# First mixer of a two-layer encoder: eight convolution taps on ScalarE, summed by adding transfers, and weight units split without VectorE

## The chip, the cores and the metric

The kernel runs on one core of one Trainium2 chip. The metric is the device time of one launch in microseconds, as the median of several runs. A profile of one further execution gives the rows below. In profiles, PE is TensorE, PEld its weight loads, DVE VectorE, ACT ScalarE, POOL GpSimd and SP SyncE, whose queue issues most transfers.

## The reference

1024 tokens of width 1024 pass two layers. Each layer is a mixer and a SwiGLU feed-forward, with a residual, scaled by 4^0.25, and a layer normalization after each:

```python
def conv_lru_mixer(x, ...):                       # layer 0
    h = x @ w_in + b_in                           # 1024 -> 4 x 512
    a_val, a_gate, b_gate, b_rec = split(h, 4)
    ya = silu(layer_norm(causal_depthwise_conv(a_val * sigmoid(a_gate), conv_w, conv_b), ...))  # 31 taps
    yb = rg_lru(causal_depthwise_conv(b_rec, lru_conv_w, lru_conv_b), ...) * gelu(b_gate)       # 4 taps
    return concatenate([ya, yb]) @ w_out
x = layer_norm(alpha * x + mixer(x), ...)         # layer 1: differential attention
x = layer_norm(alpha * x + (silu(x @ w_gate) * (x @ w_up)) @ w_down, ...)
```

All data are float32.

## The kernel before

Every matrix operand is split in two parts: `hi` is the value rounded to TensorE's fast float32 form (fp32r), made by a copy on ScalarE, and `lo` is the value less `hi`, made by a subtraction on VectorE (`split`, L569). A product is three matmuls: hi hi, hi lo, lo hi (`three`). Weights come in units of 128 x 1024 (512 KB): `load` (L551) issues the load of a unit, `ready` (L561) splits it, `prefetch` keeps up to `cap` units ahead. The first mixer loads 40 units, 24 of `win` and 16 of `wout0`.

The tokens are worked in two halves of 512. `PLAN` (L394) is the order of the steps of the first mixer:

```python
PLAN = "c0 c1 R0 R1 R2 R3 c2 L0 L1 L2 L3 c3 k3 G0 G1 G2 G3 D S x m v s o y Q0 Q1 Q2 Q3 B0 B1 B2 B3 O H0 H1 H2 H3"
```

`c` (`conv_in`, L982) multiplies value and gate for 128 channels of both halves, gates them (`glu`) and convolves the first half; `R` and `Q` are the recurrent input of the two halves with its four-tap convolution, `L` its gates, `G` and `H` the GeLU gates, `D` and `S` decay and scan, `m`, `v`, `s`, `o` mean, variance, scaling and splitting of the convolved half, `B` the 31-tap convolution of the second half, and `O` the output projection of the first half with its normalization. The feed-forward of the first half follows (`operands_a`, `ffn_lead` L1182, 18 of 22 steps), with the rest of the second half's mixer between, then mean, variance and output projection of the second half. `ffn_lead` makes two weight operands of each `up` unit: the sum of its two halves, added on GpSimd, and the second half.

`conv31` (L774) gives the last 8 to 13 of 31 taps to ScalarE or GpSimd as multiplications and adds their products on GpSimd into a page of its own; the first 18 to 23 taps are multiply-adds on VectorE into two accumulators, which two more additions join. Its pages are six halves of a fixed ring (`cring`).

SBUF is a pool of 35 pages of 128 x 1024, first free first used (`alloc` L463, `halloc` L470 for halves); a page's new user waits for all users of the old one. The order of instructions on each engine is fixed when the program is built: `solve` (L240) gives each operation a cost and a due time and lists it on its engine; a transfer issued by GpSimd is taken to hold GpSimd for 1000 ns and to begin 700 ns later. The engine then runs its list in order, and waits where an operand is not there.

Of the kernel before, what the change touches and what calls it, by code (L numbers as in the profile page):

```python
# [22 lines left out]
HALF = 512  # L23
# [3 lines left out]
HALO = 32  # L27
NSMALL = 856
# [54 lines left out]
class Order:  # L83
# [156 lines left out]
    def solve(self):  # L240
# [50 lines left out]
        while done < n:  # L291
# [29 lines left out]
            if o.dma:  # L321
                if e == "pool":
                    free[e] = s + 1000
                    b = free[e] + 700
                else:
                    free[e] = s + 60
                    hw = max(hw, s + 25) + 450
                    b = hw + 650
# [68 lines left out]
class Trunk:  # L397
    def __init__(self, tc, io, order=None, lead0=18, lead1=18, ratio1=1.65, ratio2=0.62, pool_a=(13, 13, 12, 8), pool_b=9,
                 own=(6, 6, 6, 0), ropes=2, early=3, stay=4, plan=PLAN):
# [8 lines left out]
        self.plan, self.own = plan, own  # L408
        self.pool_a, self.pool_b = pool_a, pool_b
# [8 lines left out]
        self.ahead = 1  # L418
        self.kinds = ("win", "wout0")
# [131 lines left out]
    def load(self, key):  # L551
        u = Unit(self.alloc())
        src = self.unit_src(key)

        cuts = (0, HALF, PG) if self.next_load < 2 else (0, PG)
        u.cuts = [slice(a, b) for a, b in zip(cuts, cuts[1:])]
# [4 lines left out]
    def ready(self, u):  # L561
        if u.hi is None:
            u.hi, u.lo = self.alloc(True), self.alloc(True)
            for c in u.cuts:
                self.split(self.pr(u.hi)[:, c], self.pr(u.lo)[:, c], self.pg(u.raw)[:, c])
            self.release(u.raw)
            self.unsplit -= 1

# [76 lines left out]
    def layer_norm(self, r, g, b, spread=False, store=None, parts=1):  # L645
# [7 lines left out]
        nc.gpsimd.tensor_scalar(mv[:, 2:3], mv[:, 1:2], EPS, 1.0, ALU.add, ALU.mult)  # L653
# [120 lines left out]
    def conv31(self, i, h, npool):  # L774
# [4 lines left out]
        o = self.cv(h, i)  # L779
        off = HALO * h  # L780

        def wcol(s):
            return self.vec("even_conv_w", (30 - s) * 4 + i)

        def span(s):
            a = 0 if h else s
            return slice(a, HALF), g[:, off + a - s:off + HALF - s]

        pages = [self.cring[n % len(self.cring)] for n in range(self.cnext, self.cnext + 4)]
        self.cnext += 4  # L790
        o2, p, *q = pages
        acc = [o, self.pg(o2)]
        nd = 31 - npool
        if h == 0:
            nc.vector.memset(acc[1][:, 0:1], 0.0)
            nc.gpsimd.memset(self.pg(p)[:, 0:nd], 0.0)
        for s in range(nd):
            sl, src = span(s)
            ov = acc[s % 2][:, sl]
            if s == 0:  # L800
                nc.vector.tensor_scalar(ov, src, wcol(s), self.vec("even_conv_b", i), ALU.mult, ALU.add)
            elif s == 1:
                nc.vector.tensor_scalar(ov, src, wcol(s), 0.0, ALU.mult, ALU.add)
            else:
                nc.vector.scalar_tensor_tensor(ov, src, wcol(s), ov, ALU.mult, ALU.add)
        for n, s in enumerate(range(nd, 31)):
            sl, src = span(s)
            t = self.pg(p if n == 0 else q[n % 2])[:, sl]
            if h == 0 and n < self.own[i]:
                nc.gpsimd.tensor_scalar(t, src, wcol(s), 0.0, ALU.mult, ALU.add)  # L810
            else:
                nc.scalar.activation(t, src, AF.Identity, scale=wcol(s))
            if n:
                pv = self.pg(p)[:, sl]
                nc.gpsimd.tensor_tensor(pv, pv, t, ALU.add)
        nc.vector.tensor_add(o, o, acc[1])
        nc.vector.tensor_add(o, o, self.pg(p))
# [17 lines left out]
    def conv_var(self, h):  # L835
# [4 lines left out]
        nc.gpsimd.tensor_tensor(a, v[0], v[0], ALU.mult)  # L840
# [50 lines left out]
    def lru_decay(self, h):  # L891
# [11 lines left out]
        for i in range(4):  # L903
            q = self.halloc()
            a = self.pg(self.la[i])
            nc.gpsimd.tensor_tensor(self.pg(q), a, a, ALU.mult)
# [1018 lines left out]
```

## Time and profile before

| | |
|---|---|
| median of 3 runs | 2374.13 us (2370.38 to 2376.66) |
| profiled execution, its own time | 2371.16 us |
| span of its trace | 2369.4 us |
| TensorE busy | 2195.5 us, 93% |
| VectorE busy | 1936.4 us, 82% |
| GpSimd busy | 1166.5 us, 49% |
| ScalarE busy | 981.2 us, 41% |
| mean granted TensorE clock | 0.967 of full speed |

The busy times of different engines overlap. A group of instructions is written as line, engine, operation, tile written and tiles read; nearly all have one line, since a helper records every operation. `g` are pages of the pool, `xt` the split tokens, `PS` accumulators, `SM` small columns. "x39 | 52.0, 1349 | 2.5 <-ACT" is 39 instructions, busy 52.0 us, 1349 ns each on average, and 2.5 us of idle time just before them, ended by ScalarE.

### The profile page before, as it was taken

How to read it: one execution, taken by the hardware profiler on the slowest of the kernel's cores; microseconds unless marked ns; L12 is line 12 of the kernel's file. 1: busy time of each engine (PE TensorE's matmuls, PEld its weight loads, DVE VectorE, ACT ScalarE, POOL GpSimd, SP SyncE). 2: the span in 40 equal slices, each digit the busy share in tenths (PEclk: the TensorE clock that was granted, in tenths of full speed). 3: DMA queues.
4: the chain of work that ended last, by engine and by line, in shares of the span. 5: the costliest groups of instructions: out<-in, count | busy, mean ns of one | idle time of the engine just before them, and what ended most of it. 6: DMA issues, size and time to landing. Idle time of an engine off the chain costs nothing.

```text
span 2369.4 us, 28804 instructions
## 1 busy us (share of the span) xinstructions
PE 2195.5 (93%) x9856; PEld 1760.1 (74%) x9856; DVE 1936.4 (82%) x2681; ACT 981.2 (41%) x1733; POOL 1166.5 (49%) x880
## 2 busy tenths in 40 slices
PE   9677987889999989979999998999998999999995
PEld 7566865668888868868787776677676888887884
DVE  8999997898767578987688877777779777768897
ACT  5246344433333244334344554455554333334431
POOL 4642346248766554661243435232236777656463
PEclk9888998999999999989999999899999999999998
DMA  5013233445444576756544557445436544476674
GB/s 173 31 45 116 90 131 117 151 151 219 155 150 160 187 252 157 191 132 216 175 129 152 166 173 226 133 143 169 133 98 227 189 162 157 150 230 206 177 178 129
DMA packets 149411, 374.70 MB, mean 158 GB/s; under 512 B 16144, under 2 KB 32784, under 8 KB 149264
## 3 DMA queue, kind: packets, MB, share of 16 engines
q1 hardware_dynamic: 136592, 349.78, 44.2%
q0 software_dynamic: 12672, 23.07, 5.8%
q8 instruction: 78, 1.28, 0.2%
q14 instruction: 69, 0.57, 0.1%
HBM read 291.01 MB, written 81.79 MB: 157 GB/s over the span
## 4 chain that ended last, share of the span: by engine, by line
PE 63%; DVE 20%; DMA 8%; issue 4%; POOL 2%; ACT 2%; SPq 0%; DVEq 0%; ACTq 0%; POOLq 0%
PE PS L378 63%; DVE g L378 16%; DMA g<-in_down 3%; DVE SM L378 2%; ACT g L378 2%; POOL g L378 2%; DMA g<-a_d 2%; DVE xt L378 1%; DMA g<-in_win 1%; POOL SM L378 1%; DMA z_d<-g 1%; DMA g<-in_up 0%; DMA q_d<-g 0%; DMA g<-q_d 0%; SPq L378 0%
## 5 line engine op out<-in xcount | busy, mean ns | idle before, releaser
L378 POOL TENSOR_TENSOR g<-g,g 128x512 f32<-128x512 f32 (+6 forms) x461 | 730.3, 1595 | 573.0 <-ACT g L378 293.4
L378 PE MATMUL PS<-xt,g 128*128 128x512 f32 x2416 | 624.0, 406 | 48.7 <-DVE g L378 28.4
L378 PE MATMUL PS<-g,xt 128*128 128x512 f32 (+3 forms) x2768 | 636.6, 380 | 4.1 <-DVE g L378 3.7
L378 PE MATMUL PS<-xt 128*128 128x512 f32 x2240 | 590.3, 391 | 12.4 <-ACT xt L378 8.5
L378 PEld LDWEIGHTS PS<-g,xt 128*128 128x128 f32 (+1 forms) x2768 | 504.1, 189 | 117.3 <-issue 11.7
L378 PEld LDWEIGHTS PS<-xt,g 128*128 128x128 f32 x2416 | 456.8, 193 | 167.1 <-DVE g L378 40.1
L378 DVE TENSOR_TENSOR xt<-g,xt 128x512 fp32r<-128x512 f32 x532 | 508.2, 981 | 62.9 <-ACT xt L378 59.7
L378 DVE TENSOR_TENSOR g<-g,g 128x512 f32<-128x512 f32 (+2 forms) x463 | 455.2, 997 | 71.5 <-ACT g L378 47.0
L378 ACT CAST xt<-g 128x512 fp32r<-128x512 f32 x532 | 313.7, 619 | 458.6 <-PE PS L378 274.7
L378 PEld LDWEIGHTS PS<-xt 128*128 128x128 f32 x2240 | 420.5, 188 | 105.8 <-ACT xt L378 10.6
L378 DVE TENSOR_TENSOR g<-PS,g 128x512 f32<-128x512 f32 (+3 forms) x408 | 257.8, 641 | 175.4 <-POOL g L378 81.9
L378 POOL TENSOR_TENSOR g<-g 128x512 f32<-128x512 f32 x153 | 231.2, 1528 | 264.6 <-DMA g<-in_gate 119.5
L378 PE MATMUL PS<-g,g 128*128 128x512 f32 (+6 forms) x984 | 257.9, 387 | 54.2 <-ACT g L378 25.3
L378 ACT CAST g<-g 128x512 fp32r<-128x512 f32 (+1 forms) x247 | 187.1, 771 | 287.4 <-DVE g L378 101.8
L378 PE MATMUL PS<-xt,xt 128*128 128x512 f32 (+4 forms) x736 | 255.6, 400 | 3.0 <-ACT xt L378 1.2
L378 PEld LDWEIGHTS PS<-g,g 128*128 128x128 f32 (+1 forms) x984 | 172.6, 193 | 100.0 <-ACT g L378 27.1
L378 DVE SCALAR_TENSOR_TENSOR g<-g,SM,g 128x1024 f32<-128x1024 f32 (+9 forms) x215 | 241.2, 1133 | 5.9 <-POOL SM L378 3.1
L378 ACT ACTIVATE g<-PS,SM 128x512 f32<-128x512 f32 (+8 forms) x266 | 179.3, 688 | 153.3 <-PE PS L378 95.0
L378 PEld LDWEIGHTS PS<-xt,xt 128*128 128x128 f32 (+1 forms) x736 | 135.6, 190 | 43.1 <-issue 12.2
L378 PE MATMUL PS<-SM,g 128*128 128x128 f32 (+1 forms) x704 | 115.6, 281 | 26.7 <-DVE g L378 16.2
L378 PEld LDWEIGHTS PS<-SM,g 128*128 128x128 f32 x704 | 91.4, 158 | 49.7 <-DVE g L378 17.1
L378 POOL DMA_DIRECT2D g<-in_down x88 | 79.0, 951 | 97.4 <-DMA g<-in_down 88.4
(48 smaller groups left out, 1101.4 us busy)
## 6 DMA issues: line engine op xcount, KB each, us to landing
g<-in_up SPq DMA_DIRECT2D x88, 512.0 KB, 4.4
g<-in_down SPq DMA_DIRECT2D x176, 256.0 KB, 3.3
z_d<-g SPq DMA_DIRECT2D x44, 512.0 KB, 3.6
g<-z_d SPq DMA_DIRECT2D x44, 512.0 KB, 4.2
g<-in_gate SPq DMA_DIRECT2D x44, 512.0 KB, 4.2
g<-in_down POOLq DMA_DIRECT2D x88, 256.0 KB, 6.5
a_d<-g SPq DMA_DIRECT2D x36, 512.0 KB, 4.8
g<-a_d SPq DMA_DIRECT2D x36, 512.0 KB, 5.9
```

The source lines that it names most:

```text
L378: r = f(*a, **k)
```

## The change

- `conv31`: the same for both halves and all channels. ScalarE makes the products of the first eight taps, each in a temporary half page from the pool; the first is written into the accumulator with the bias, the other seven are added into it by transfers from SBUF to SBUF, issued by GpSimd (`accum_op=ALU.add`). The other 23 taps are VectorE's. The fixed ring has four halves instead of six, and `conv31` of the first half stands one product later.
- `ready`: for all units but the first two of the first mixer, ScalarE writes `hi` and then `-hi` into `lo`, and a transfer issued by GpSimd adds the raw unit (512 KB) to `lo`.
- `ffn_lead`, in both layers: the sum of the two halves of an `up` unit is made by an adding transfer from DRAM (256 KB) into the first half.
- The square in `conv_var` and the four in each `lru_decay` move from GpSimd to ScalarE, and the addition of epsilon in `layer_norm` from GpSimd to VectorE.
- The planner takes a transfer issued by GpSimd to begin 1500 ns after its issue instead of 700.

```diff
@@ Order.solve
                 if e == "pool":
                     free[e] = s + 1000
-                    b = free[e] + 700
+                    b = free[e] + 1500
@@ Trunk.load
         u = Unit(self.alloc())
+        u.adding = self.adding
...
+        if self.next_load == 1:
+            self.adding = True
@@ Trunk.ready
             u.hi, u.lo = self.alloc(True), self.alloc(True)
+            if u.adding:
+                self.split_adding(u)
+                self.unsplit -= 1
+                return
...
+    def split_adding(self, u):
+        nc = self.nc
+        nc.scalar.copy(self.pr(u.hi), self.pg(u.raw))
+        nc.scalar.mul(self.pr(u.lo), self.pg(u.hi), -1.0)
+        nc.gpsimd.dma_start(self.pg(u.lo), self.pg(u.raw), accum_op=ALU.add)
+        self.release(u.raw)
@@ Trunk.layer_norm
-        nc.gpsimd.tensor_scalar(mv[:, 2:3], mv[:, 1:2], EPS, 1.0, ALU.add, ALU.mult)
+        nc.vector.tensor_scalar(mv[:, 2:3], mv[:, 1:2], EPS, 1.0, ALU.add, ALU.mult)
@@ Trunk.conv31 (NTAP = 8)
+        acc = [self.cv(h, i)] + [self.pg(self.cring[(self.cnext + n) % len(self.cring)]) for n in range(2)]
+        self.cnext += 2
...
+        for s in range(NTAP):
+            sl, src, w = tap(s)
+            if s == 0:
+                nc.scalar.activation(acc[0], src, AF.Identity, bias=self.vec("even_conv_b", i), scale=w)
+                continue
+            t = self.halloc()
+            nc.scalar.activation(self.pg(t)[:, sl], src, AF.Identity, scale=w)
+            nc.gpsimd.dma_start(acc[0][:, sl], self.pg(t)[:, sl], accum_op=ALU.add)
+            self.release(t)
+        for s in range(NTAP, 31):
+            n = s - NTAP
+            sl, src, w = tap(s)
+            ov = acc[1 + n % 2]
+            if n < 2:
+                if h == 0:
+                    nc.vector.memset(ov[:, 0:s], 0.0)
+                nc.vector.tensor_scalar(ov[:, sl], src, w, 0.0, ALU.mult, ALU.add)
             else:
-                nc.vector.scalar_tensor_tensor(ov, src, wcol(s), ov, ALU.mult, ALU.add)
-        for n, s in enumerate(range(nd, 31)):
-            sl, src = span(s)
-            t = self.pg(p if n == 0 else q[n % 2])[:, sl]
-            if h == 0 and n < self.own[i]:
-                nc.gpsimd.tensor_scalar(t, src, wcol(s), 0.0, ALU.mult, ALU.add)
-            else:
-                nc.scalar.activation(t, src, AF.Identity, scale=wcol(s))
-            if n:
-                pv = self.pg(p)[:, sl]
-                nc.gpsimd.tensor_tensor(pv, pv, t, ALU.add)
-        nc.vector.tensor_add(o, o, acc[1])
-        nc.vector.tensor_add(o, o, self.pg(p))
+                nc.vector.scalar_tensor_tensor(ov[:, sl], src, w, ov[:, sl], ALU.mult, ALU.add)
+        nc.vector.tensor_add(acc[1], acc[1], acc[2])
+        nc.vector.tensor_add(acc[0], acc[0], acc[1])
@@ Trunk.conv_var
-        nc.gpsimd.tensor_tensor(a, v[0], v[0], ALU.mult)
+        nc.scalar.activation(a, v[0], AF.Square)
@@ Trunk.lru_decay
-            nc.gpsimd.tensor_tensor(self.pg(q), a, a, ALU.mult)
+            nc.scalar.activation(self.pg(q), a, AF.Square)
@@ Trunk.layer0_in
-        self.cring = [self.halloc() for _ in range(6)]
+        self.cring = [self.halloc() for _ in range(4)]
@@ Trunk.conv_in
         self.glu(i, 0, bv, bg)
-        self.conv31(i, 0, self.pool_a[i])
         bv = self.bank()
         self.colmul(bv, uv, 1)
+        self.conv31(i, 0)
         bg = self.bank()
@@ Trunk.ffn_lead
             pu, u1, u2 = self.raw("up", l, f)
-            w2, w4 = self.w_operand(u1, u2), self.w_operand(u2)
+            nc.gpsimd.dma_start(u1, self.io["up"][l][f][:, HALF:], accum_op=ALU.add)
+            w2, w4 = self.w_operand(u1), self.w_operand(u2)
@@ Trunk.emit, ahead of layer 1's first loads
                 self.cap = 4
+                self.adding = False
```

## Rows read from the trace of the kernel before

**Rows 1.** Page, part 1: busy us of each engine, share of the span, instructions.

```profile
PE 2195.5 (93%) x9856; PEld 1760.1 (74%) x9856; DVE 1936.4 (82%) x2681; ACT 981.2 (41%) x1733; POOL 1166.5 (49%) x880
```

**Rows 2.** Table by stretch: start:end, length, engines' busy us, clock, DMA share, GB/s.

```profile
0.00:95.00 95.00, 89.60 (x382) 73.29 (x383) 87.77 (x100) 43.72 (x60) 55.01 (x44) 1.00 0.35 121
95.00:181.00 86.00, 51.63 (x203) 40.53 (x201) 84.75 (x116) 30.24 (x43) 39.15 (x27) 0.78 0.12 37
181.00:290.00 109.00, 95.80 (x395) 75.45 (x394) 103.01 (x132) 53.55 (x68) 34.94 (x26) 0.94 0.33 111
290.00:429.00 139.00, 110.03 (x434) 84.02 (x432) 123.67 (x136) 67.34 (x109) 71.59 (x48) 0.89 0.33 118
429.00:546.00 117.00, 108.13 (x495) 84.79 (x494) 104.73 (x143) 47.50 (x88) 44.56 (x35) 1.00 0.50 184
546.00:800.00 254.00, 254.00 (x1123) 210.38 (x1122) 186.04 (x232) 87.72 (x152) 173.53 (x115) 1.00 0.47 159
```

**Rows 3.** Chain that ended last, in order of time: start, us, what.

```profile
115.50 17.47 DVE g L378 x16
...
145.87 16.40 DVE g L378 x16
```

**Rows 4.** Timeline of TensorE: start, us, operation, count, [idle before it, releaser].

```profile
5.40 89.46 PE L378 MATMUL PS<-xt,g 128*128 128x512 f32 x380 [5.40 <-ACT g L378]
...
123.33 1.22 PE L378 MATMUL PS<-g,g 128*128 128x512 f32 x2 [22.99 <-ACT g L378]
...
227.66 42.20 PE L378 MATMUL PS<-g,xt 128*128 128x512 f32 x184 [3.13 <-DVE g L378]
```

**Rows 5.** Groups on VectorE by form, 0:546: count, busy us, mean ns, idle before.

```profile
L378 DVE TENSOR_TENSOR g<-g,g 128x1024 fp32r<-128x1024 f32 x39 | 52.0, 1349 | 2.5 <-ACT g L378 2.1 <-PE PS L378 0.2
L378 DVE SCALAR_TENSOR_TENSOR g<-g,SM,g 128x512 f32<-128x512 f32 x52 | 51.8, 997 | 0.3
...
L378 DVE SCALAR_TENSOR_TENSOR g<-g,SM 128x512 f32<-128x512 f32 x40 | 38.0, 959 | 0.0
...
L378 DVE SCALAR_TENSOR_TENSOR g<-g,SM,g 128x503 f32<-128x503 f32 x4 | 6.3, 1576 | 0.0
...
L378 DVE SCALAR_TENSOR_TENSOR g<-g,SM,g 128x507 f32<-128x507 f32 x4 | 4.8, 1192 | 0.0
```

**Rows 6.** Timeline of all engines, 146:150.

```profile
146.72 0.74 DVE L378 SCALAR_TENSOR_TENSOR g<-g,SM 128x510 f32<-128x510 f32 x1
147.24 2.97 POOL L378 TENSOR_TENSOR g<-g,g 128x488 f32<-128x488 f32 x2 [8.79 <-ACT g L378]
...
149.04 1.72 DVE L378 SCALAR_TENSOR_TENSOR g<-g,SM 128x508 f32<-128x508 f32 x1
```

**Rows 7.** Timeline of all engines, 913:915.

```profile
913.63 0.86 POOL L378 DMA_DIRECT2D g<-in_down  x1 [2.35 <-DMA g<-in_down]
913.79 1.28 DVE L378 TENSOR_TENSOR xt<-g,xt 128x512 fp32r<-128x512 f32 x2
```

**Rows 8.** Groups on GpSimd by form, 0:546.

```profile
L378 POOL TENSOR_TENSOR g<-g,g 128x512 f32<-128x512 f32 x47 | 74.2, 1584 | 95.7 <-ACT g L378 75.6 <-PE PS L378 17.8 <-DVE g L378 0.6
L378 POOL TENSOR_TENSOR g<-g 128x512 f32<-128x512 f32 x39 | 58.3, 1505 | 79.5 <-DMA g<-in_up 46.7 <-ACT g L378 9.3 <-DVE xt L378 7.2
...
L378 POOL TENSOR_SCALAR SM<-SM 128x1 f32<-128x1 f32 x8 | 7.5, 940 | 42.8 <-DVE SM L378 42.4
```

**Rows 9.** Groups on ScalarE by form, 0:546.

```profile
L378 ACT CAST g<-g 128x1024 fp32r<-128x1024 f32 x39 | 40.3, 1048 | 48.4 <-DVE g L378 25.6 <-PE PS L378 8.2 <-DMA g<-in_wout 6.8
```

**Rows 10.** GpSimd's adding transfers from in_down, 800:850: us to landing.

```profile
DMA to landing us min/median/max: 4.1/6.7/8.2
```

**Rows 11.** Page, parts 3 and 6: queues; issues, KB each, us to landing.

```profile
q1 hardware_dynamic: 136592, 349.78, 44.2%
q0 software_dynamic: 12672, 23.07, 5.8%
...
g<-in_down POOLq DMA_DIRECT2D x88, 256.0 KB, 6.5
```

More of the change, by code (lines that the diff above doesn't have):

```diff
@@ L27 @@
 HALO = 32
+NTAP = 8
 NSMALL = 856
@@ L397, with __init__ @@
 class Trunk:
-    def __init__(self, tc, io, order=None, lead0=18, lead1=18, ratio1=1.65, ratio2=0.62, pool_a=(13, 13, 12, 8), pool_b=9,
-                 own=(6, 6, 6, 0), ropes=2, early=3, stay=4, plan=PLAN):
+    def __init__(self, tc, io, order=None, lead0=18, lead1=18, ratio1=1.65, ratio2=0.62, ropes=2, early=3, stay=4, plan=PLAN):
         self.dry = order is None
@@ L407, in __init__ @@
         self.ropes, self.early, self.stay = ropes, early, stay
-        self.plan, self.own = plan, own
-        self.pool_a, self.pool_b = pool_a, pool_b
+        self.plan = plan
         self.order = [] if self.dry else order
@@ L772, in ge, with conv31, tap @@
         return self.pg(self.xpage(h, i))[:, HALF:]
-    def conv31(self, i, h, npool):
+    def conv31(self, i, h):
         nc = self.nc
         g = self.pg(self.Y[h][i])
-        o = self.cv(h, i)
         off = HALO * h
-        def wcol(s):
-            return self.vec("even_conv_w", (30 - s) * 4 + i)
-        def span(s):
+        acc = [self.cv(h, i)] + [self.pg(self.cring[(self.cnext + n) % len(self.cring)]) for n in range(2)]
+        self.cnext += 2
+        def tap(s):
             a = 0 if h else s
[L787 to L797, printed above, removed]
-            sl, src = span(s)
-            ov = acc[s % 2][:, sl]
-            if s == 0:
-                nc.vector.tensor_scalar(ov, src, wcol(s), self.vec("even_conv_b", i), ALU.mult, ALU.add)
-            elif s == 1:
-                nc.vector.tensor_scalar(ov, src, wcol(s), 0.0, ALU.mult, ALU.add)
-            else:
-                nc.vector.scalar_tensor_tensor(ov, src, wcol(s), ov, ALU.mult, ALU.add)
-        for n, s in enumerate(range(nd, 31)):
-            sl, src = span(s)
-            t = self.pg(p if n == 0 else q[n % 2])[:, sl]
-            if h == 0 and n < self.own[i]:
-                nc.gpsimd.tensor_scalar(t, src, wcol(s), 0.0, ALU.mult, ALU.add)
-            else:
-                nc.scalar.activation(t, src, AF.Identity, scale=wcol(s))
-            if n:
-                pv = self.pg(p)[:, sl]
-                nc.gpsimd.tensor_tensor(pv, pv, t, ALU.add)
-        nc.vector.tensor_add(o, o, acc[1])
-        nc.vector.tensor_add(o, o, self.pg(p))
@@ new lines, in tap @@
+            return slice(a, HALF), g[:, off + a - s:off + HALF - s], self.vec("even_conv_w", (30 - s) * 4 + i)
+        for s in range(NTAP):
+            sl, src, w = tap(s)
+            if s == 0:
+                nc.scalar.activation(acc[0], src, AF.Identity, bias=self.vec("even_conv_b", i), scale=w)
[4 more added lines that the diff above has]
+            self.release(t)
@@ L957, in layer0_in @@
             "L": lambda i: self.lru_gate(i, 0),
[L958 removed]
+            "B": lambda i: self.conv31(i, 1),
             "D": lambda i: self.lru_decay(0),
@@ L1814, in late_in @@
                 self.cap = 4
+                self.adding = False
                 self.kinds = ("v", "qk", "wout1")
```

1 line of the change is left out of this document (removed).

## The prediction

> **What bounds the kernel now.** I read the page first, for the share of each engine [rows 1]: TensorE is busy 93% of the span and VectorE 82%. That average hides the stage that the change touches, so the second view is the table by stretch [rows 2]. From 546 us on TensorE is busy in every microsecond shown, at full clock: 1123 matmuls in 254 us, 0.226 us each. Before 546 us it isn't. I price each stretch at 0.226 us a matmul, and the 128-column transposes (32 in 290:429, 80 in 429:546) at about half of it, 0.13: the stretches need 86, 46, 89, 95 and 104 us and take 95, 86, 109, 139 and 117. With 5 us for the first loads and 3 for eight whole-precision matmuls counted in, TensorE loses some 118 us, of which 40 lie in 95:181, 20 in 181:290 and 44 in 290:429. VectorE is busy 504 of the 546 us there. The chain of waits [rows 3] says the same: between 95 and 200 us it runs through VectorE, sixteen operations at a time, and TensorE once stands still for 23 us [rows 4].
>
> Why VectorE is full is to be seen in its groups and its timeline [rows 5, 6]. A convolution tap of nearly the same length takes 0.74 us or 1.72 us. It is long exactly while GpSimd runs its adds; twelve groups of four taps have means from 1.19 to 1.58 us. Beside a transfer that GpSimd issues, a two-input operation stays short: two in 1.28 us [rows 7]. So GpSimd's adds cost VectorE nearly as much time as they save it.
>
> **The change part by part.** *VectorE.* Taken away: GpSimd's 74 adds, 18 multiplications and 18 feed-forward adds in this stage (1.5 to 1.6 us for an add [rows 8]), and with them what they cost VectorE. The twelve long groups alone carry 32 us over 0.73 us a tap (with means spread evenly over that range, 48 taps at 0.65). The full-width taps of rows 5 stand at about 0.98 instead of 0.74 (92 operations, 22 us). Some 170 other two-input operations at the same 0.24 us give 41 us, an estimate: 95 us in all. Also away: the subtraction for 38 of the 40 weight units, some 1.23 us once it is not held up (1.35 on average now [rows 5]), 47 us. Added: the taps go from 166 to 184, 18 x 0.74 = 13 us, and eight small normalization steps, 1 us. VectorE falls from 504 to about 376 us, below the 430 that TensorE needs. It stops being the bound.
>
> *ScalarE.* It has 64 taps as before, but 38 negated copies at 1.05 us [rows 9], 40 us, and ten squares, 6 us. It is busy 242 of 546 us in rows 2, so this is covered; without the cover it would be 46 us. *GpSimd.* It loses about 190 us and issues 112 transfers at 0.86 us [rows 7], 96 us.
>
> *The chain of adding transfers.* Here the cost sits. The seven transfers of a convolution all add into one page, so each must have landed before the next is issued, and GpSimd waits in order, with the weight units' and the feed-forward's transfers queued behind. No row shows an adding transfer from SBUF. The nearest are the 256 KB ones from `down`: 4.1 us at the shortest and 8.2 at the longest in one stretch [rows 10], 6.5 as the median [rows 11]. I take 5.5 us a link, between the shortest and the median: the stage uses 0.12 to 0.35 of the DMA engines up to 429 us where 546:800 uses 0.47 [rows 2], but the change adds traffic. The Trainium skill, "DMA: Bandwidth & Descriptors", section "Anatomy of one DMA — SWDGE (gpsimd) path", gives about 2.0 us and the bytes at 436 GB/s, an estimate of 2.6 us for 256 KB; by it the output projection below would start at 170 us and the kernel take some 2269. The rows differ from it, and the rows decide.
>
> The temporaries of the taps come from the pool of 35 pages, first free first used. Going through the allocations, 16 pages are free where the second half's convolutions (B0 to B3) begin, all last used by the rec units Q0 to Q3. 28 temporaries go round these 16, and the pages handed out next are those of the last taps: output units 1 and 2 get the pages of B2's last links and B3's first, unit 3 those of B3's third and fourth link, which is the tenth link after B0's first. So the weights of the output projection wait for a chain of ten links.
>
> Now the times. The first 380 matmuls end at 94.9 us today, nearly without a wait [rows 4]. If the next 72 (the gates L and half of c3) follow at 0.226, the last gated column is ready at T = 111 us. Its own chain of seven links ends at T + 38, and its mean is ready at T + 43; TensorE has 240 matmuls (54 us) to do meanwhile, so this wait is covered up to 7 us a link. Q0 is done at about T + 27. Ten links (55 us), two ScalarE steps (2.1 us) and a 512 KB adding transfer (5.5 + 1.6, since the software queue's 5.8% of the span is 1.56 us for each of its 88 transfers [rows 11]) put the last output unit at T + 91 = 202, say 203 us. The projection's 192 matmuls end at 247 instead of 269.9 [rows 4]: 23 us, less 3 for a clock that starts low after the idle time (0.78 in 95:181 [rows 2], between the levels of 1.2 and 2.4 GHz): 20 us gained.
>
> From 290 to 429 us TensorE loses 44 us, with VectorE busy 124 of 139. The bounds are 0 and 44; I take 20 of them back: VectorE is freed, but each raw page of the feed-forward is held one link longer. Eight to ten pages are free there and four go into each step of 5.4 us, so a page comes round after two steps, and a delay of 5.5 us is just covered. In 429:546, 3 of the lost 13 us. At the end of the kernel each normalization loses a GpSimd step of 0.94 us [rows 8], 1 us on the path. In layer 1's feed-forward 22 adds become transfers: nothing, as attention's work covers them, with 10 us either way if it does not. The planner's higher price for GpSimd's transfers reorders the 88 in the down-projections: 3 us either way.
>
> Sum: 20 + 20 + 3 + 1 = 44 us. The profiled execution took 2371.2 us, 3 below the median of the runs, so 2371.2 - 44 + 3 = 2330.
>
> **The rivals.** *The chain is covered.* If links take 4.1 us, the last output unit is there at T + 76 = 187, the projection ends at 231, and with the feed-forward free of waits all 44 us of 290:429 return: 39 + 44 + 3 + 1 = 87, time 2287. For it: a source in SBUF and few other transfers. Against it: only the shortest row is that short, and GpSimd waits in order.
>
> *The gain is eaten.* At 10 us a link the projection ends at 295, 25 later than now, which takes all that the rest gives: 2375. The 8.2 us of rows 10 lies close, and a plan that assumes shorter links puts other work behind each wait.
>
> *Slower: the DMA engines become the bound of the first mixer.* By rows 2 they are busy 184 of the 546 us. The change adds 56 + 18 transfers of 256 KB at 1.56 us and 38 of 512 KB at 3.1 us, 233 us. Together 417 us, below the 500 that the stage is to take. It decides from a price 1.55 times as high (2.4 us for 256 KB) on: then 546 us are full. At 1.75 times the stage takes 592 us and the kernel 2420. For it: an adding transfer reads its target too, and the software queue moves 23.07 MB in 5.8% where the hardware queue moves 349.78 in 44.2% [rows 11], half the rate. Against it: the price comes from adding transfers already.
>
> A smaller danger, without a share of its own, lies in the order on VectorE. The Trainium skill, "SBUF — State Buffer", section "SBUF: two separate sides", says that a GpSimd transfer's descriptors wait while VectorE runs a copy-like operation in a two-port mode. Rows 7 have no such operation, so no row here shows it.
>
> **How the numbers follow.** My forecast, a gain of 20 to 70 us, gets 0.55; its own range is 2304 to 2354. The covered chain gets 0.18, the eaten gain 0.13, the DMA bound 0.14. A measurement of this kernel tells 0.3%, 7 us, from no change. Faster is 0.55 + 0.18 = 0.73, same 0.13, slower 0.14. Links of 4.1 us with everything regained, and 10 us in layer 1 besides, give 2277; links of 8.2 us (5 lost at the projection, 3 for the clock) with only 5 regained after it give 2377. The range is 2275 to 2380; it leaves out most of the slower case.
>
> **What would show it.** Right: in 95:290 VectorE's taps at 0.74 us and its busy share under 80%; an idle time of TensorE of 20 to 40 us ahead of the output projection, released by a weight unit that waited for an adding transfer; stretches after 546 us moved but not changed. Wrong: TensorE idle before many weight units (GpSimd's order), a DMA share near 0.9 (the DMA bound), no wait ahead of the projection (the covered chain), or a longer first feed-forward.

## The result and the profile after

The changed kernel takes 2403.34 us (median of four runs) against 2375.39 for the kernel before on the same chip: ratio 1.0129, 95% interval 1.011 to 1.0148. It is 28 us slower. The forecast was 45 us faster, and its range ended at 2380.

Page of the changed kernel, part 1 (engines, answers to [rows 1]) and part 3 (queues, answers to [rows 11]):

```profile
PE 2215.3 (92%) x9856; PEld 1772.5 (74%) x9856; DVE 1809.7 (75%) x2697; ACT 1026.4 (43%) x1783; POOL 1057.4 (44%) x836
...
q1 hardware_dynamic: 136592, 349.78, 43.6%
q0 software_dynamic: 32544, 69.16, 16.9%
```

VectorE has lost 127 us of work, as intended, and the software queue moves three times the bytes. The table by stretch (columns as in [rows 2]):

```profile
0.00:95.00 95.00, 78.81 (x324) 63.68 (x325) 63.97 (x140) 52.41 (x74) 21.06 (x28) 0.98 0.82 201
95.00:181.00 86.00, 68.37 (x276) 53.09 (x275) 43.53 (x70) 45.87 (x59) 20.50 (x23) 0.88 0.59 125
181.00:290.00 109.00, 60.40 (x207) 45.18 (x205) 77.29 (x116) 62.24 (x85) 38.55 (x41) 0.75 0.83 182
290.00:429.00 139.00, 129.88 (x556) 101.79 (x557) 89.03 (x139) 54.78 (x83) 28.45 (x29) 0.97 0.73 186
429.00:546.00 117.00, 103.30 (x441) 82.23 (x440) 82.73 (x123) 57.39 (x93) 27.67 (x26) 0.93 0.61 170
```

In 181:290 neither TensorE (60 of 109 us) nor VectorE (77) is full. The DMA engines are, nearly: 0.83 of the time, 0.33 before. TensorE's granted clock is 0.75 there, between its levels of 1.2 and 2.4 GHz, and it stands still again and again. Its timeline shows where (columns as in [rows 4]); the output projection begins at 221 us:

```profile
11.34 15.52 PE L379 MATMUL PS<-xt,g 128*128 128x512 f32 x55 [11.34 <-ACT xt L379]
...
154.38 1.22 PE L379 MATMUL PS<-xt,g 128*128 128x512 f32 x2 [11.47 <-ACT g L379]
...
193.84 1.22 PE L379 MATMUL PS<-xt,g 128*128 128x512 f32 x2 [6.34 <-ACT g L379]
...
231.04 6.32 PE L379 MATMUL PS<-g,xt 128*128 128x512 f32 x17 [6.85 <-DMA g<-g]
249.46 3.62 PE L379 MATMUL PS<-g,xt 128*128 128x512 f32 x8 [12.11 <-ACT g L379]
263.77 19.44 PE L379 MATMUL PS<-g,xt 128*128 128x512 f32 x72 [10.69 <-DMA g<-g]
292.22 5.76 PE L379 MATMUL PS<-g,xt 128*128 128x512 f32 x14 [9.01 <-DMA g<-g]
```

The 23 us of [rows 4] are gone; in their place stand six waits for a unit or its adding transfer. The chain of waits shows what stands ahead of the matmul at 299 us: a tap's transfer, the load that waited for its page, copy, negated copy, the unit's transfer.

```profile
275.84 4.67 DMA g<-g
...
280.56 3.52 DMA g<-in_wout
...
284.16 1.05 ACT g L379
...
285.24 1.06 ACT g L379
...
286.59 12.57 DMA g<-g
...
299.20 30.94 PE PS L379 x134
```

The unit's transfer took 12.57 us to land. Issues of the changed kernel in 181:290 (KB each, median us to landing), and for comparison one of the kernel before in the same stretch:

```profile
g<-g POOLq DMA_DIRECT2D x28, 256.0 KB, 6.2
g<-g POOLq DMA_DIRECT2D x10, 512.0 KB, 7.1
g<-in_wout SPq DMA_DIRECT2D x8, 512.0 KB, 5.5
```

```profile
g<-in_wout SPq DMA_DIRECT2D x11, 512.0 KB, 3.8
```

VectorE's taps did become short (groups by form, 0:546; [rows 5] has 997 and 1576 ns):

```profile
L379 DVE SCALAR_TENSOR_TENSOR g<-g,SM,g 128x512 f32<-128x512 f32 x96 | 65.8, 746 | 0.4
...
L379 DVE SCALAR_TENSOR_TENSOR g<-g,SM,g 128x501 f32<-128x501 f32 x4 | 2.9, 737 | 0.0
```

All kernels here issue the same 9856 matmuls in nearly the same order, so the start of the n-th one is a milestone. From each trace I took that start less the one of the kernel before (us, to within 0.3, each from its own first operation; the 700th is about the first of the output projection, the 900th lies just behind its end):

```
n-th matmul            0   300   500   700   900  1000  1400  1800  4100  6200  7700  9800
before, start at     5.4  76.3 154.6 222.4 271.3 293.7 426.0 520.4  1073  1533  1848  2336
after               +5.9 +13.2 -18.2  -1.0 +46.9 +45.7 +12.2 +25.9 +12.4  +9.6 +28.4 +33.5
b_behind_o          +0.2 +12.2 -20.5  +3.8 +20.5 +42.6 +13.3 +27.5 +15.0 +14.3 +32.8 +35.9
taps_ring           +6.8 +16.2 -15.6  +6.6 +65.4 +67.4 +34.6 +46.0 +30.0 +28.8 +49.1 +53.1
units_vector        +0.2  +1.1 -31.5 -15.4  +7.2  +6.0 -16.8 -15.0 -25.0 -25.7  -1.1  -1.3
units_shadow        +0.1  +6.5 -22.5  +5.7 +46.1 +44.9 +15.3 +25.5 +15.4 +15.3 +37.7 +40.0
shadow_small        +0.2  +0.8 -32.0 -10.2 +17.2 +16.1  -8.7  -7.2 -17.1 -17.8  +4.6  +7.3
b_vector            +0.3 +10.7 -22.2  +1.8  +3.8  +2.3 -24.1 -16.7 -29.4 -27.8  -5.7  -2.8
lead_gpsimd         +6.0 +15.6 -14.8  +7.9 +53.1 +56.3 +29.8 +31.9 +21.0 +17.0 +15.7 +14.0
two_undone          +0.1  +2.3 -30.4 -19.3  +2.4  +1.1 -25.8 -26.0 -36.3 -40.2 -40.0 -36.9
two_undone_ring     +3.3  +3.5 -28.4 -16.2 +17.1 +15.8 -13.3  -9.8 -23.5 -27.8 -28.5 -27.3
two_undone_behind   +0.2  +2.0 -30.7 -26.3 -13.7  +0.8 -18.1 -15.3 -27.8 -30.5 -31.2 -25.2
two_undone_b_vector +0.1  -0.0 -32.9 -26.2 -29.7 -31.0 -54.9 -51.4 -62.2 -62.9 -63.7 -62.9
two_undone_all_vector +0.1 -0.4 -32.7 -24.6 -27.9 -29.2 -47.2 -38.8 -48.8 -49.2 -49.2 -45.2
two_chains_held     +0.1  +2.9 -29.9 -15.7  +3.7  +2.5  +1.2  -0.9 -12.6 -14.9 -16.0 -15.6
```

The changed kernel loses 13 us in its first 300 matmuls, wins 31 up to the 500th, loses 65 from there to the 900th, wins 21 up to the 1800th and 11 in layer 0's down-projection, and loses 19 in layer 1's feed-forward lead and 5 at the end.

### The profile page after: what moved, and what is told of

Its sections match the earlier page's. It is cut to its first block, busy times and chain, and to the rows that moved or that the text cites. A ratio compares the mean times of both kernels' runs of the same rounds, so it can differ in the third digit from the quotient of the medians.

```text
span 2400.3 us, 29019 instructions
## 1 busy us (share of the span) xinstructions
PE 2215.3 (92%) x9856; PEld 1772.5 (74%) x9856; DVE 1809.7 (75%) x2697; ACT 1026.4 (43%) x1783; POOL 1057.4 (44%) x836
## 4 chain that ended last, share of the span: by engine, by line
PE 57%; DMA 13%; DVE 11%; issue 3%; ACT 2%; POOL 1%; SPq 0%; DVEq 0%; POOLq 0%; ACTq 0%
PE PS L379 57%; DVE g L379 7%; DMA g<-in_up 5%; DMA g<-in_down 2%; DVE xt L379 2%; ACT g L379 2%; DVE SM L379 2%; POOL g L379 1%; DMA g<-g 1%; DMA g<-a_d 1%; DMA z_d<-g 1%; DMA g<-in_wout 0%; ACT xt L379 0%; DMA q_d<-g 0%; DMA g<-x_d 0%
## 5 line engine op out<-in xcount | busy, mean ns | idle before, releaser
L379 POOL TENSOR_TENSOR g<-g,g 128x512 f32<-128x512 f32 (+1 forms) x365 | 581.0, 1607 | 436.0 <-ACT g L379 189.6
L379 PE MATMUL PS<-g,xt 128*128 128x512 f32 (+2 forms) x2768 | 655.5, 387 | 51.5 <-DMA g<-g 31.1
L379 PEld LDWEIGHTS PS<-g,xt 128*128 128x128 f32 (+1 forms) x2768 | 514.3, 193 | 170.4 <-DMA g<-g 34.5
L379 DVE TENSOR_TENSOR xt<-g,xt 128x512 fp32r<-128x512 f32 x532 | 518.3, 1000 | 86.2 <-ACT xt L379 80.7
L379 DVE TENSOR_TENSOR g<-g,g 128x512 f32<-128x512 f32 (+2 forms) x423 | 380.8, 913 | 133.9 <-ACT g L379 89.4
L379 PE MATMUL PS<-g,g 128*128 128x512 f32 (+5 forms) x984 | 254.7, 384 | 19.8 <-ACT g L379 9.8
L379 POOL TENSOR_TENSOR g<-g 128x512 f32<-128x512 f32 x121 | 187.0, 1560 | 180.4 <-DMA g<-in_gate 117.2
L379 DVE SCALAR_TENSOR_TENSOR g<-g,SM,g 128x512 f32<-128x512 f32 (+19 forms) x310 | 260.4, 884 | 3.1 <-POOL SM L379 0.9
L379 POOL DMA_DIRECT2D g<-g x94 | 83.0, 936 | 245.0 <-ACT g L379 143.8
L379 ACT ACTIVATE g<-g 128x512 f32<-128x512 f32 (+1 forms) x142 | 104.8, 744 | 139.7 <-DVE g L379 122.5
```

Source lines behind the costliest of these rows:

```text
L379: r = f(*a, **k)
```

## The experiments

Times are medians; ratios are to the kernel before on the same chip, with the 95% interval. Differences between two experiments are of medians. Every edit is to the changed kernel unless it says otherwise. Theory 1 is the one of the prediction: pages last used by the second half's tap temporaries. Theory 2 is load: the bytes on the DMA engines. Theory 3 is GpSimd's order. Theory 4 is the path: the copies and the transfer between a unit's load and its first matmul.

**b_behind_o: the second half's convolutions behind the projection.**

```diff
-PLAN = "c0 c1 R0 R1 R2 R3 c2 L0 L1 L2 L3 c3 k3 G0 G1 G2 G3 D S x m v s o y Q0 Q1 Q2 Q3 B0 B1 B2 B3 O H0 H1 H2 H3"
+PLAN = "c0 c1 R0 R1 R2 R3 c2 L0 L1 L2 L3 c3 k3 G0 G1 G2 G3 D S x m v s o y Q0 Q1 Q2 Q3 O B0 B1 B2 B3 H0 H1 H2 H3"
```

> The four convolutions of the second half are written behind the output projection in the plan, so that the projection's units, rows and gains take pages whose last users are the rec units and not the taps' temporaries. Nothing else is changed. Theory 1 (pages): the projection no longer waits for the taps' chains; its waits of 6.9, 10.7, 9.0 us and most of the 12.1 us go, the last of its matmuls moves from 316 us to 270 to 280, and the kernel gains 20 to 45 us on the changed kernel: 2358 to 2383. Theory 2 (the DMA engines are full in the first mixer): the same bytes cross in the same stretch, the weights still come late, the projection ends past 300 us and the time stays within 8 us of 2403. Theory 3 (GpSimd's order, made by a planner that prices an adding transfer too low): between the two, since the weight units still queue on GpSimd behind convolution links: a gain of 8 to 20 us.

Measured: 2403.12, ratio 1.0127 (1.0099 to 1.0155). Theory 1's mechanism is there: the 900th matmul comes 26 us sooner. But at the 1000th only 3 us of it are left, and the gain of theory 1 is nil. The time is what theory 2 had expected; the projection's end, ahead of 292 us, is not (past 300). TensorE now waits behind the projection (timeline):

```profile
287.15 2.37 PE L379 MATMUL PS<-SM,g 128*128 128x128 f32 x8 [13.37 <-DVE SM L379]
...
300.75 1.22 PE L379 MATMUL PS<-xt,g 128*128 128x512 f32 x2 [7.77 <-ACT g L379]
```

**taps_ring: temporaries in pages of their own.** The same question without a new order.

```diff
+        if i == 0:
+            self.want[False] += 4
         self.conv31(i, 1)
+        if i == 3:
+            self.trim({False: self.want[False] - 4, True: self.want[True]})
```

> As the changed kernel, but the 28 temporaries of the second half's convolutions go round four pages taken for them (eight half pages) in place of all 16 free ones, so that rows, gains and units 0 to 2 of the output projection take pages last used by the rec units. The order of the plan is as it was. Theory 1 (pages): the loads of the projection's units no longer wait for convolution links; the projection's last matmul comes at 275 to 295 us in place of 316, and, if what follows does not wait for the same chains, the kernel takes 2365 to 2385. Theory 2, as it stands after the convolutions moved behind the projection gained 27 us at the projection and lost them again right behind it: the adding transfers of this stretch (28 taps, 16 units) take their 70 us wherever they stand, and the kernel stays within 8 us of 2403.

Measured: 2422.72, ratio 1.0195 (1.0165 to 1.0226), 19 slower than the changed kernel. The projection's loads start earlier now (the fourth at 227.6 us instead of 250.9) and it waits all the same (timeline of TensorE):

```profile
287.26 5.29 PE L379 MATMUL PS<-g,xt 128*128 128x512 f32 x16 [32.34 <-DMA g<-g]
```

The unit whose transfer it waits for stands behind nine tap links in a row in GpSimd's queue, and its negated copy (281.21) begins only when a link has landed (issued at 275.74, landed at 281.14). So not all of the projection's pages are free of the taps here. Theory 1's remedy, as far as it goes, does not gain.

**price_4500: a truer latency in the planner.**

```diff
-                    b = free[e] + 1500
+                    b = free[e] + 4500
```

> Only the planner's latency for a GpSimd transfer goes from 1500 to 4500 ns (with issue and bytes it then counts 6.2 us for 256 KB; 6.2 us is the median of the adding taps in 181:290). Theory 3 (the order on GpSimd and ScalarE is made for transfers that land in 3.2 us): 15 to 40 us come back, 2363 to 2388, with the projection's end at 275 to 300. Theory 1 (pages): the projection has to wait for the same ten links, whatever order they stand in; its end stays at 305 to 320 and the time within 10 us of 2403. Theory 2 (DMA engines full): no change, 2403 within 8.

Measured: 2420.75, ratio 1.0206 (1.0185 to 1.0228), 17 slower: 0.6 us behind the kernel before at the 500th matmul, where the changed kernel is 18 ahead. Theory 3's remedy, a higher price, does not gain; none of the three theories had expected a loss.

**units_vector: units split on VectorE again.**

```diff
-        if self.next_load == 1:
-            self.adding = True
```

> The low part of the mixer's weight units is made by a VectorE subtraction again; the taps' and the feed-forward's adding transfers stay. This takes 38 adding transfers of 512 KB away (19.9 MB, 58% of what the change adds to the software queue before 546 us) and 38 negated copies on ScalarE. Theory 1 (pages): the projection's units still take the pages of the taps' temporaries; of the 46 us that the projection's end lost, 15 to 25 come back (the transfer and the copy behind each page wait), and VectorE gets 47 us of work more: 2380 to 2400. Theory 2 (DMA engines full): with more than half of the added bytes gone the DMA share of 95:290 falls under 0.6 and both the 12 us at the start and the 46 us at the projection come back: 2345 to 2365. Theory 3 (GpSimd's order): the units leave GpSimd's queue, so the start's 12 us and about half of the projection's loss come back: 2365 to 2385.

Measured: 2362.88, ratio 0.9947 (0.992 to 0.9974), 40 faster than the changed kernel. The 12 us of the start are back, and by the 900th matmul all 40, as theory 2 says. What remains between the 500th and 900th matmul is 39 us. The chain of waits shows theory 1's link in it: a tap's transfer, the load that waited for its page, the copy, TensorE.

```profile
252.21 7.57 DMA g<-g
...
259.83 4.64 DMA g<-in_wout
...
264.49 1.05 ACT g L379
...
265.59 34.30 PE PS L379 x156
```

**units_shadow and shadow_small: is it the path or the load?** VectorE makes the low part; the transfer goes to a scratch in DRAM that nothing reads, whole, then a sixteenth of it (which the planner still prices as the whole).

```diff
-        nc.gpsimd.dma_start(self.pg(u.lo), self.pg(u.raw), accum_op=ALU.add)
+        self.nc.gpsimd.dma_start(self.s_d[n % 4], self.pg(u.raw), **kw)
```

```diff
+        self.nc.gpsimd.dma_start(self.s_d[n % 4][:, :64], self.pg(u.raw)[:, :64], **kw)
```

> The low part of a unit is made by VectorE, but the 38 transfers of 512 KB are still issued on GpSimd from the same raw page, into a scratch in DRAM that nothing reads (the first four write, the others add), and the raw page is held until they have read it. No matmul waits for them. Theory 2 (load: the DMA engines and GpSimd's in-order queue carry too much): most of the 40 us that the units' adding transfers cost come back as a loss, 2390 to 2410. Theory 4 (the path: copy, negated copy, transfer of 6 to 12 us stand between the load of a unit and its first matmul): nothing waits for them any more, so the time is that of the run with units split on VectorE, 2363 to 2372.

> As the run with the units' 38 idle transfers into a scratch, but each moves 64 of the 1024 columns, a sixteenth of the bytes; its place in GpSimd's order, its waits for the unit's load and the raw page it holds are kept, and the planner prices it as the whole one. Theory 2a (bytes: the DMA engines of the first mixer carry too much, and taps, units and loads land late): the loss goes, 2360 to 2375. Theory 2b (GpSimd waits in order: a convolution link stands behind a unit's transfer that waits for its load, and the tap chains come late): the loss stays, 2395 to 2410.

Measured: 2408.77, ratio 1.0128 (1.0089 to 1.0167), and 2375.54, ratio 0.9994 (0.9977 to 1.0011). No matmul waits for a shadow, yet the whole ones cost all that the real ones did: theory 4, the path, is out, and with it ScalarE's negated copies, which neither run has. With the bytes cut, 33 us of it go. The other 13 us to units_vector were not taken apart: GpSimd's places and waits, the raw page held, and the load of the small transfers are what is left. Tables by stretch, whole and small:

```profile
0.00:95.00 95.00, 84.57 (x354) 68.56 (x355) 75.30 (x150) 49.41 (x71) 21.74 (x30) 0.98 0.83 212
...
181.00:290.00 109.00, 63.45 (x210) 47.90 (x210) 81.05 (x114) 54.77 (x78) 37.45 (x42) 0.73 0.81 179
```

```profile
0.00:95.00 95.00, 89.04 (x379) 72.66 (x380) 80.90 (x160) 54.04 (x78) 24.36 (x33) 1.00 0.71 176
...
181.00:290.00 109.00, 74.73 (x276) 57.42 (x275) 91.33 (x130) 46.21 (x65) 38.75 (x44) 0.81 0.75 168
```

**b_vector: all 31 taps of the second half on VectorE.**

```diff
-        for s in range(NTAP):
+        nt = 1 if h else NTAP
+        for s in range(nt):
```

> The changed kernel with one thing altered: the second half's convolutions do all 31 taps on VectorE, so 28 adding transfers go and 32 taps come to VectorE (24 us; it is busy 166 of 248 us in 181:429). If these transfers are the cause at the projection, most of the 65 us between the 500th and 900th matmul come back, 40 or more, and the kernel takes 2345 to 2375, of which the 20 us that the first feed-forward regains today are given up again. If the units' own bytes are the cause, 10 to 22 us come back: 2380 to 2393.

Measured: 2359.55, ratio 0.9946 (0.9926 to 0.9966), 44 faster than the changed kernel. Of the 65 us between the 500th and the 900th matmul 39 go. The 26 that stay equal what the units' removal took from the same stretch (65 less 39), so the two causes add up: second-half taps 39, units 26. With both removed (two_undone_b_vector below, which has the feed-forward's sums on GpSimd besides) 3 us of the 65 are left.

**lead_gpsimd: the feed-forward's sums on GpSimd again.**

```diff
-            nc.gpsimd.dma_start(u1, self.io["up"][l][f][:, HALF:], accum_op=ALU.add)
-            w2, w4 = self.w_operand(u1), self.w_operand(u2)
+            w2, w4 = self.w_operand(u1, u2), self.w_operand(u2)
```

> In the first part of the feed-forward the sum of the two halves of an up unit is made by GpSimd again, not by an adding transfer from memory; all else as changed. If the 18 us that the changed kernel falls behind in layer 1's lead come from these transfers, they come back: 2385 within 6. If they come from the planner's other order, nothing changes beyond 6 us. In the first layer's lead the rival says that GpSimd's adds lengthen VectorE's operations again and up to 10 us of the 35 regained there are lost, so that the sum is 2393.

Measured: 2384.87, ratio 1.0049 (1.0031 to 1.0067), 18 faster than the changed kernel. From the 6200th to the 7700th matmul the changed kernel loses 19 us and this one gains 1. Up to the 1800th it is 6 us behind the changed kernel, as the rival said, if less. In the changed kernel the chain of waits there runs through the load and then the adding load, one behind the other on one page:

```profile
1529.80 7.03 DMA g<-in_up
...
1537.45 7.56 DMA g<-in_up
```

**two_undone: units_vector and lead_gpsimd together.**

> Both parts whose undoing gained alone are undone together: the units' low parts come from VectorE, the feed-forward's sums from GpSimd. What stays of the change: the taps made by ScalarE and summed by adding transfers, the squares on ScalarE, the normalization step on VectorE and the planner's price. If the two losses are separate (40 us before 546 us, 18 us in layer 1) the sum is 2403 - 40 - 18 = 2345, within 8. If GpSimd's feed-forward adds lengthen VectorE's work again, where VectorE now also has the subtractions, 10 to 15 us of it are lost: 2355 to 2360.

Measured: 2330.94, ratio 0.9812 (0.9782 to 0.9842). The losses are separate, and the sum came out 14 better than expected; up to the 1800th matmul the sums on GpSimd lose nothing here (it is 11 us further on than units_vector).

**two_undone_ring, two_undone_behind: theory 1 again, with less load.** The edits are those of taps_ring and b_behind_o.

> As the run with two parts undone, and the second half's tap temporaries go round four pages of their own. There the chain of waits ran from the taps' transfers through the load of an output unit to TensorE (a load issued at 259.8 us behind a transfer that took 7.57). Theory 1 (pages) expects the projection 15 to 30 us earlier and a time of 2315 to 2335. Theory 2 (the transfers take their time wherever they stand): within 8 us of the run with two parts undone.

> Units' low parts by VectorE, feed-forward sums by GpSimd, and the second half's convolutions behind the output projection in the plan. With two parts undone the kernel is 31 us ahead of the kernel before at the 500th matmul and 2 us behind it at the 900th. Theory 1 (pages of the taps' temporaries), in what is left of it: the projection no longer waits for the taps, 15 to 25 us of these 33 come back, 2306 to 2318. If the taps' transfers only push their wait on to the feed-forward, as in the run with this move alone: 2325 to 2340.

Measured: 2346.48, ratio 0.9875 (0.984 to 0.991), and 2343.97, ratio 0.9859 (0.9833 to 0.9886): 16 and 13 slower than two_undone. In the first the projection ends 15 us later than in two_undone, and it is no full test of theory 1: the load of its last unit still begins when a tap's transfer lands (chain of waits):

```profile
254.88 3.31 DMA g<-g
...
258.32 3.52 DMA g<-in_wout
```

In the second the projection runs through without a wait, 16 us sooner, and the next thing waits. TensorE's timeline and, below it, those of GpSimd and ScalarE:

```profile
198.65 41.99 PE L379 MATMUL PS<-g,xt 128*128 128x512 f32 x184 [0.38 <-DVE g L379]
255.27 2.10 PE L379 MATMUL PS<-SM,g 128*128 128x128 f32 x7 [14.63 <-DVE g L379]
```

```profile
249.15 1.53 POOL L379 TENSOR_TENSOR SM<-SM 128x1 f32<-128x1 f32 x1 [3.43 <-DVE SM L379]
```

```profile
254.07 1.34 ACT L379 ACTIVATE g<-g,SM 128x512 f32<-128x512 f32 x2 [6.75 <-DMA g<-g]
255.55 1.05 ACT L379 CAST g<-g 128x1024 fp32r<-128x1024 f32 x1
```

TensorE stands still 14.6 us while the projected rows are normalized. GpSimd's small step in this does not wait for the taps: it waits for VectorE. In two_undone TensorE has 94 gate matmuls to do behind the projection (271.9 to 293.4); here the copy of the next gate unit, on ScalarE, stands behind two tap products that waited 6.75 us for a tap's transfer to land. So the taps hold more than the projection's pages: what is freed there is lost at the next thing that stands behind them.

**two_undone_b_vector, two_undone_all_vector: fewer transfers still.** The first adds b_vector's edit to two_undone, the second has `NTAP = 1` in both halves.

> Two parts undone, and the second half's convolutions do all 31 taps on VectorE: 28 adding transfers fewer (7.3 MB), 32 taps more on VectorE, at 0.74 us 24 us of work between 180 and 429 us where it is busy 209 of 248 us. If the 33 us lost between the 500th and the 900th matmul come from the taps' transfers and the pages they hold, 15 to 30 come back and 5 to 10 are lost to VectorE: 2308 to 2325. If VectorE is the bound there: 2340 to 2355.

> No adding transfer is left in the first mixer: units by VectorE, feed-forward sums by GpSimd, and both halves' convolutions with one tap on ScalarE and 30 on VectorE. Against the run that keeps the first half's taps on transfers, VectorE gets 28 taps and a few sums more, some 22 us, in 0:181, where it is busy 168 of 181 us there. If VectorE is the bound there, 15 to 25 us are lost: 2324 to 2334. If the first half's transfers cost as much as the taps save, 2309 within 6.

Measured: 2309.08, ratio 0.972 (0.9699 to 0.974), the fastest of all, 66 faster than the kernel before; and 2322.03, ratio 0.9784 (0.9754 to 0.9814). The first half's 28 transfers pay: 13 us. They do not pay where they run, as had been expected (in 0:181): at the 1000th matmul the two kernels are 2 us apart, at the 1800th 13. Table by stretch of the first:

```profile
0.00:95.00 95.00, 89.50 (x383) 72.83 (x384) 85.04 (x153) 54.73 (x78) 15.04 (x21) 1.00 0.65 173
95.00:181.00 86.00, 68.94 (x280) 53.84 (x279) 82.85 (x122) 50.95 (x66) 19.47 (x17) 0.90 0.39 101
181.00:290.00 109.00, 104.90 (x463) 85.64 (x462) 103.06 (x151) 39.78 (x57) 15.10 (x9) 0.97 0.38 121
290.00:429.00 139.00, 121.58 (x494) 94.77 (x494) 127.70 (x165) 60.97 (x93) 33.78 (x20) 0.95 0.40 140
429.00:546.00 117.00, 108.60 (x506) 86.99 (x505) 104.00 (x142) 43.30 (x87) 73.23 (x51) 1.00 0.55 194
```

VectorE is as busy as in [rows 2] (503 us against 504), but it does more of the taps in that time (834 ns each at 512 columns, 997 in [rows 5]), it is 51 us further on by the 1800th matmul, and TensorE has 463 matmuls in 181:290 where the changed kernel had 207.

**two_undone_700, before_1500: the planner's price alone.**

```diff
-                    b = free[e] + 1500
+                    b = free[e] + 700
```

before_1500 makes the reverse edit in the kernel before.

> Two parts undone, and the planner's latency of a GpSimd transfer back from 1500 to 700 ns. Every run at 1500 or more gains 9 to 18 us on the kernel before in the down-projection of layer 0. If this gain comes from the price alone, it goes: 2331 + 10 = 2341, and the first mixer moves by less than 5 us either way. If it came from elsewhere, 2331 within 6.

> The kernel before with one number altered, the planner's latency of a GpSimd transfer from 700 to 1500 ns; all its 88 such transfers are the adding loads of the down-projections. If the price alone gives what the down-projection of layer 0 gained in every run at 1500 or more, 9 to 18 us: 2358 to 2367. If it only helps a kernel whose other transfers it prices too: 2376 within 6.

Measured: 2352.85, ratio 0.9903 (0.9877 to 0.9929), 22 slower than two_undone, twice what had been expected: 10 lost up to the 1800th matmul, 5 more up to the 4100th. And 2367.8, ratio 0.9974 (0.9955 to 0.9993): 4 to 6 faster than the kernel before by itself; its trace gains 11.5 us between the 2900th and the 4100th matmul and gives them back by the 7700th.

**two_chains, two_chains_held: bytes or chain?** To two_undone: the second half's taps add into two pages in turn.

```diff
+            to = ev if h and s % 2 else acc[0]
-            nc.gpsimd.dma_start(acc[0][:, sl], self.pg(t)[:, sl], accum_op=ALU.add)
+            nc.gpsimd.dma_start(to[:, sl], self.pg(t)[:, sl], accum_op=ALU.add)
```

> The run with two parts undone, and the second half's taps add into two pages in turn (the second page's first tap is written by ScalarE itself, and VectorE adds the two pages at the end: four operations of 0.7 us more). 24 of 28 transfers remain, but a link waits only for the link before the last. If the chain (each link waiting for the one before, GpSimd in order behind it) is what costs 33 us between the 500th and the 900th matmul, about half of it comes back: 2310 to 2320. If the bytes and the pages of these transfers cost it, a seventh of it comes back at most: 2325 to 2333.

> As the run with two chains, but the second page of each convolution is kept until the feed-forward's first part is done, and VectorE joins the sums there, so that no page of the projection has VectorE's last tap as its last user (four pages fewer are free meanwhile). If the chain of links is what costs the 33 us between the 500th and the 900th matmul: 10 to 20 us less than the run with two parts undone, 2310 to 2322. If the bytes and the pages they hold cost it: 2325 to 2340. If VectorE, which is then asked to do its taps early, is the wait: over 2345.

Measured: 2359.68, ratio 0.9948 (0.9923 to 0.9972), and 2354.24, ratio 0.9915 (0.9888 to 0.9941), both slower than two_undone. The first tells nothing of the question: its pages came free only after VectorE's last operation, and TensorE waited for VectorE, which was full in 181:290 (timeline, table):

```profile
262.00 17.11 PE L379 MATMUL PS<-g,xt 128*128 128x512 f32 x64 [19.80 <-DVE g L379]
```

```profile
181.00:290.00 109.00, 49.30 (x162) 35.45 (x162) 108.79 (x160) 44.02 (x61) 24.64 (x26) 0.71 0.61 145
```

The second does, up to the 900th matmul: the last tap is issued at 235 us instead of 249 and the projection ends no sooner (+3.7 against +2.4). It then falls 26 us behind two_undone up to the 1400th, with four pages fewer; that these are the cause was not tried. Its time is the one expected if VectorE were the wait (over 2345); VectorE is busy 94.7 of 109 us in 181:290, as in two_undone (95.0).

## Why the prediction was wrong

**VectorE: right.** It is busy 357 us of the first 546 (forecast 376, before 504), with taps at 0.75 us.

**The price and the length of a transfer: right.** The software queue takes 41.9% of 546 us, 229 us (forecast 233 for the added transfers), and the DMA engines are busy 392 us (forecast 417); a link of the second half takes 6.2 us as median (forecast 5.5 between 4.1 and 8.2), one of the first half 3.5. What the price does was judged wrongly. I compared the sum with the whole stage and let the DMA engines decide from 1.55 times the price on. The units' bytes cost 33 us at the forecast price. The stage is not even: 0.72 as a mean, but 0.82 in 0:95 and 0.83 in 181:290, and there loads and links alike land late. The sign of that rival came true, by a smaller mechanism than it named: the stage is not full, it is nearly full where a transfer has somebody waiting.

**The failed step: "Q0 is done at about T + 27", with TensorE's matmuls as the clock of everything up to the projection.** The working gives the 500th matmul at 122, the 700th at 167 and the projection's end at 247 us; they came at 136, 221 and 318 (the 900th). The first 14 us go with the units' transfers (123 in units_vector, 132 in units_shadow, where no matmul waits for them). Between the 500th and the 700th I had 45 us of matmuls; it took 85. The stretch in the changed kernel, in the kernel before and in two_undone_all_vector (columns as in [rows 2]):

```profile
136.41:221.38 84.97, 56.21 (x201) 41.14 (x199) 51.28 (x75) 61.36 (x81) 27.36 (x28) 0.80 0.63 134
```

```profile
154.78:222.41 67.63, 53.64 (x202) 40.61 (x200) 65.40 (x82) 39.40 (x52) 20.93 (x14) 0.85 0.24 82
```

```profile
122.09:197.76 75.67, 55.92 (x201) 41.72 (x200) 73.94 (x117) 50.29 (x64) 8.45 (x6) 0.82 0.23 77
```

In the changed kernel TensorE is busy 56 us of it, at a granted clock of 0.80, and waits 26, of which 23 are for ScalarE. The longest wait (11.47 us, at 154.38) is for a unit whose load (149.69) begins when a link of the first half's convolutions has landed (issued at 141.74, landed at 149.57): the first half's temporaries hold pages too, and the working has no such wait. Without any adding transfer there (two_undone_all_vector) the stretch takes 76 us, but then VectorE is busy 74 of them; so how much of the 40 us the transfers cost is not shown. TensorE, which I had priced as the bound there, is the bound in none of the three.

So the chain of ten links, which I started at 138, starts late: the second half's first tap is issued at 201.6 us in the changed kernel and at 174.5 in two_undone, 64 and 37 us late. In the changed kernel the projection's fourth unit gets its last page 65 us after that (forecast: ten links, 55 us): its negated copy waits for a link that lands at 266.98 (timeline of ScalarE).

```profile
267.01 1.06 ACT L379 ACTIVATE g<-g 128x1024 fp32r<-128x1024 f32 x1 [4.20 <-DMA g<-g]
```

The projection ends about 70 us late, and 25 in two_undone. The date was wrong by 64 us and the chain's length by 10. One wait was put at nothing: the projection's second four units. Three of their loads (275.36, 280.56, 289.76) each begin when one of the last three links lands, and TensorE waits 10 us for these units. The sign given for being right, 20 to 40 us of idle time at the projection behind units that waited for an adding transfer, came true (40 us from 221 to 316); it does not tell when the chain began.

**The pages: the mechanism right, the remedy not.** The projection's units do wait for the taps' pages, and moving the convolutions shows that they hold the projection up, by 26 us here and 16 in two_undone. But what is freed is lost again just behind it, where other work stands behind the taps. Of the remedies tried, only taking the transfers away pays: 44 us in b_vector, 22 from two_undone to two_undone_b_vector. Whether their bytes or the pages and orders that they hold weigh more stays open; the length of each chain is not it, as far as two_chains_held shows.

**After the projection: right.** 21 us are regained from the 900th to the 1800th matmul (forecast 23).

**Two sizes off.** Layer 1's feed-forward transfers, put at nothing with 10 us either way, cost 18 to 19: attention's work does not cover two loads in series on one page. The planner's price, put at 3 us either way, gives 11 us in layer 0's down-projection and 22 in two_undone. At the end of the kernel the normalization was to give 1 us and 5 are lost; but before_1500 loses 2 there with the old normalization, and units_vector and lead_gpsimd, with the new one, lose nothing, so no cost of its own is shown.

**The sum.** The profiled span grew by 31 us where the sum said 44 less, 75 in all: 67 at the projection (20 ahead became 47 behind), 2 behind it, 19 in layer 1's lead and 6 at the end, less 16 won between the 1800th and the 6200th matmul and 3 behind the 9800th. The three undoings that gain alone (40, 44 and 18 us) would make 2301; together they measure 2309.

## What to carry to other kernels

Work taken from a full engine and given to DMA is paid for where the DMA engines are already busy: price it by stretch, not over the stage, and ask who waits for the loads that now land later. A chain of dependent transfers needs a start date from what really holds it, and whatever lies behind it in an in-order queue or in a page's order moves with it. A mixed change is best taken apart on the chip: here three of its parts together cost 94 us (2403 to 2309), and the rest was worth 66.

## What had not been expected

The same adding transfer of 252 to 256 KB from SBUF lands in 3.2 to 3.4 us where the DMA engines are 0.34 busy (most of units_vector's in 95:181) and in 6.2 us, as median, at 0.83 (the changed kernel's in 181:290). The Trainium skill, "DMA: Bandwidth & Descriptors", section "Anatomy of one DMA — SWDGE (gpsimd) path", gives about 2.0 us and the bytes at 436 GB/s, an estimate of 2.6 us; no run here shows one so short (the shortest takes 3.24 us).

A sixteenth of the bytes is not a sixteenth of the load: shadow_small's 32 KB transfers still take 3.8 us to land, and with 13 of them and one tap more the software queue holds the DMA engines for 44.1% of 181:290, where units_vector has 37.2%.

Giving the planner a latency nearer to the measured one made things worse (4500 ns in the changed kernel: 17 us), giving it a shorter one did too (700 ns in two_undone: 22 us).
